# A streaming log-softmax: two places at which SyncE empties its store queue before the next load

## The chip, the cores and the metric

One NeuronCore of one Trainium2 chip runs the kernel. The metric is the device time of one execution in microseconds (us); the figure for a kernel is the median of several runs. A separate, profiled execution gives the trace that the views below come from.

## The reference

The input x is float32 of shape 16 x 512 x 50000: 8192 rows of 50000 values, 1.64 GB. The result has the same shape.

```python
def reference(x: np.ndarray) -> np.ndarray:
    max_x = np.max(x, axis=-1, keepdims=True)
    shifted = x - max_x
    log_sum_exp = np.log(np.sum(np.exp(shifted), axis=-1, keepdims=True))
    return (shifted - log_sum_exp).astype(np.float32)
```

## The kernel before

**Tiles.** A tile is 32 rows. Each row is cut into 4 parts of 12500 values, and each part lies on a partition of its own, so that a tile fills 128 partitions x 12500 float32 (50,000 bytes per partition, 6.4 MB). There are 256 tiles and 4 buffers of that size (`bufs[0]` to `bufs[3]`); tile t lives in buffer t mod 4. A tile is loaded, worked on in place, and stored from the same buffer.

**What happens to a tile.** VectorE waits for the load (`landed[j]`, L45 called by `whole`). It takes the negated maximum of each partition in 4 pieces of 3125 columns (L206). While it does, ScalarE takes the exponential of each finished piece with that piece's maximum as the bias, and sums it (L242). VectorE brings the 4 partitions of a row to one maximum with two small transposes (L174 to L189). ScalarE makes the factors that bring the pieces' sums to that maximum (L250), VectorE multiplies (L217), TensorE adds the 4 partitions of a row with a matrix of ones (L270), ScalarE takes the logarithm (L236), and VectorE subtracts maximum and logarithm from the whole tile in one pass (L194), which increments `subtracted[j]`. For the last tile this pass is made in 4 pieces.

**Who issues the transfers.** All loads and stores are issued by SyncE, in an order written out by hand, on one hardware queue that feeds 16 DMA engines; each engine carries 8 of the 128 partitions of every transfer. A load (L145) increments `landed[j]` by 16, one for each DMA engine; a store (L149) first waits for `subtracted[j]` and increments `stored[j]` by 16. `take` (L43 to L45) waits until a semaphore has a value and takes that value off again.

**The order.** SyncE loads tiles 0 to 3 and stores tile 0. Then come 63 rounds of 4 steps each (L155 to L160). Step j of round q stores tile 4q + 1 + j from the next buffer k, waits until the store from buffer j (tile 4q + j) has landed, and loads tile 4q + 4 + j into buffer j:

```python
            for j in range(NBUF):
                k = (j + 1) % NBUF
                store(k, dst(q, j), bufs[k])
                take(sync, stored[j])
                load(j, src(q, j))
```

After the rounds SyncE stores tiles 253 and 254, stores tile 255 in 4 pieces of 12500 bytes per partition, and waits for the stores that are still under way. The other engines have loops of their own of 63 rounds; only the semaphores tie them to SyncE.

Of the kernel before, what the change touches and what calls it, by code (L numbers as in the profile page):

```python
# [17 lines left out]
R = P // G  # L18
C = 3125
NBUF = 4  # L20

NS = 4

# [19 lines left out]
def take(engine, sem, n=16):  # L43

    engine.wait_ge(sem, n).then_inc(sem, -n)  # L45


def cols(c):
    return slice(c * C, (c + 1) * C)
# [3 lines left out]
def kernel(  # L53
# [11 lines left out]
    ntiles = N // R  # L65


    rounds = (ntiles - NBUF) // NBUF
    assert ntiles % NBUF == 0 and rounds >= 2

    xt = xf.rearrange("(t r) (g w) -> t (r g) w", r=R, g=G)
    ot = of.rearrange("(t r) (g w) -> t (r g) w", r=R, g=G)

    def run(a, first, n):

        part = a[first : first + NBUF * n].rearrange("(q i) p w -> q i p w", i=NBUF)
        return lambda q, i: part[bass.ds(q, 1), i].rearrange("o p w -> (o p) w")
# [12 lines left out]
    ones = consts.tile([P, P], FP32, name="ones")  # L90
    bufs = [data.tile([P, W], FP32, name=f"buf{j}") for j in range(NBUF)]
    dump = dump_pool.tile([P, C], FP32, name="dump")
    sums = sum_pool.tile([P, NBUF], FP32, name="sums")
    rowsums = [sums[:, k : k + 1] for k in range(NBUF)]

# [15 lines left out]
    def sem(name):  # L111
        return ctx.enter_context(nc.semaphore(name))

    landed = [sem(f"landed{j}") for j in range(NBUF)]
    stored = [sem(f"stored{j}") for j in range(NBUF)]
# [13 lines left out]
    @block.gpsimd  # L129
    def _(gpsimd):  # L130
        view = ones.rearrange("p (r g) -> p r g", g=G)
        gpsimd.memset(ones, 1.0).then_inc(ready)  # L132
        gpsimd.affine_select(  # L133
            out=view, in_=view, pattern=[[-G, R], [0, G]], base=0,
            channel_multiplier=1, compare_op=ALU.is_ge, fill=0.0,
        ).wait_op(ready, 1, "sem-ge").then_inc(ready)
        gpsimd.affine_select(  # L137
            out=view, in_=view, pattern=[[G, R], [0, G]], base=G - 1,
            channel_multiplier=-1, compare_op=ALU.is_ge, fill=0.0,
        ).wait_op(ready, 2, "sem-ge").then_inc(ready)  # L140

    @block.sync
    def _(sync):
        def load(j, src):
            sync.dma_start(out=bufs[j], in_=src).then_inc(landed[j], 16)  # L145

        def store(j, dst, buf):
            take(sync, subtracted[j], 1)
            sync.dma_start(out=dst, in_=buf).then_inc(stored[j], 16)  # L149

        for t in range(NBUF):
            load(t, xt[t])
        store(0, ot[0], bufs[0])
        src, dst = run(xt, NBUF, rounds), run(ot, 1, rounds)
        with sync.Fori(0, rounds) as q:  # L155
            for j in range(NBUF):
                k = (j + 1) % NBUF
                store(k, dst(q, j), bufs[k])
                take(sync, stored[j])
                load(j, src(q, j))  # L160
        for j in range(1, NBUF - 1):
            store(j, ot[ntiles - NBUF + j], bufs[j])
        for c in range(NS):
            store(NBUF - 1, ot[ntiles - 1][:, cols(c)], bufs[NBUF - 1][:, cols(c)])
        for j in range(NBUF - 1):
            take(sync, stored[j])
        take(sync, stored[NBUF - 1], 16 * NS)
# [147 lines left out]
```

## Time and profile before

| | us |
|---|---|
| median of 5 runs | 7593.89 |
| lowest and highest of the 5 | 7593.56, 7594.41 |
| the profiled execution | 7595.35 |
| its span, from the first to the last instruction | 7593.6 |
| VectorE busy (72% of the span) | 5440.7 |
| ScalarE busy (42%) | 3184.7 |
| TensorE busy (6%) | 477.9 |
| one load, from issue to landing, median | 44.2 |
| one store, from issue to landing, median | 47.8 |

How to read it: the page first gives the busy time of each engine and then the span in 40 equal slices, where a digit is the busy share of a slice in tenths; the DMA line is the mean busy share of the 16 DMA engines, and the GB/s line is what they moved. HBM is read with 1638.40 MB and written with 1638.40 MB, which is 432 GB/s over the span. In a line on a group of instructions, the name after L is a line of the kernel, `out<-in` are its tiles, and behind the bar stand the busy time, the mean length of one in ns, and the idle time of the engine just before them, with what ended it. DVE is VectorE, ACT ScalarE, PE TensorE, SP SyncE; a name with a q (DVEq, SPq) is that engine's sequencer. The line on the chain of waits follows the work that ended last back from the end; in this execution it covers only the last 46 us, from 7547.38 to the end of the last pass of VectorE.

### The profile page before, as it was taken

Reading aid. Unit: us, or ns where it says so; the run is one execution under the profiler, and the core shown is the slowest. Engines: PE = TensorE matmul, PEld = TensorE weight load, DVE = VectorE, ACT = ScalarE, POOL = GpSimd, SP = SyncE. Lnnn points to the kernel's source line nnn. Section 1 sums busy time; section 2 is a strip of 40 time slices with the busy share of each in tenths; the row PEclk is TensorE's granted clock in tenths of the full one; section 3 lists DMA queues with packets and bytes.
Section 4 is the critical chain, followed back from the end, with each engine's and each line's share of the span. In section 5 each row is a group of like instructions: output and inputs, shape, how many; then the busy total and the mean of one; then the engine's idle time right before and its main releaser. Section 6 shows DMA issues by size and latency. Waiting matters only on the chain. (4 is left out here: it accounts for less than half of the span.)

```text
span 7593.6 us, 14139 instructions
## 1 busy us (share of the span) xinstructions
PE 477.9 (6%) x2048; PEld 456.0 (6%) x2048; DVE 5440.7 (72%) x2819; ACT 3184.7 (42%) x2561; POOL 1.4 (0%) x7
## 2 busy tenths in 40 slices
PE   0000000000000000000000000000000000000000
PEld 0000000000000000000000000000000000000000
DVE  7777777777777777777777777777777777777776
ACT  4444443434444344443444434444344443444433
POOL 0000000000000000000000000000000000000000
DMA  9999999999999999999999999999999999999998
GB/s 425 431 432 433 432 433 433 434 432 433 433 434 432 433 434 433 432 433 433 433 432 433 433 432 433 433 433 433 432 433 434 433 432 432 434 433 432 432 434 386
DMA packets 74162, 3276.85 MB, mean 432 GB/s; under 512 B 8240, under 2 KB 8240, under 8 KB 8240
## 3 DMA queue, kind: packets, MB, share of 16 engines
q1 hardware_dynamic: 74160, 3276.83, 99.9%
q14 instruction: 2, 0.02, 0.0%
HBM read 1638.40 MB, written 1638.40 MB: 432 GB/s over the span
## 5 line engine op out<-in xcount | busy, mean ns | idle before, releaser
L242 ACT ACTIVATE dump<-buf,negm 128x3125 f32<-128x3125 f32 x1024 | 2937.2, 2868 | 3806.3 <-DVE negm L206 3708.8
L206 DVE TENSOR_REDUCE negm<-buf 128x1 f32<-128x3125 f32 x1024 | 3418.3, 3400 | 924.6 <-DVEq L45 924.6
L194 DVE TENSOR_SCALAR buf<-buf,negmax,logsum 128x12500 f32<-128x12500 f32 (+1 forms) x259 | 1738.9, 6715 | 553.8 <-ACT logsum L236 553.8
L270 PE MATMUL sums<-scaled,ones 128*128 128x1 f32 x2048 | 477.9, 355 | 7088.5 <-DVE scaled L217 7088.5
L270 PEld LDWEIGHTS sums<-scaled,ones 128*128 128x128 f32 x2048 | 456.0, 328 | 7110.4 <-DVE scaled L217 7110.4
L217 DVE TENSOR_TENSOR scaled<-scale,part 128x4 f32<-128x4 f32 x256 | 41.7, 163 | 580.2 <-ACT scale L250 580.2
L236 ACT ACTIVATE logsum<-sums 128x1 f32<-128x1 f32 x256 | 43.9, 171 | 551.0 <-PE sums L270 551.0
L242 ACT ACTIVATION_READ_ACCUMULATOR dump<-buf,negm 128x1 f32 x1024 | 190.8, 186 | 0.0
L250 ACT ACTIVATE scale<-negm,negmax 128x4 f32<-128x4 f32 x256 | 76.1, 297 | 23.6
L211 DVE TENSOR_REDUCE negp<-negm 128x1 f32<-128x4 f32 x256 | 40.2, 157 | 39.2 <-DVE negm L206 39.2
L189 DVE STREAM_TRANSPOSE negmax<-spread 128x32 f32<-128x32 f32 x256 | 54.2, 212 | 8.9
L174 DVE STREAM_TRANSPOSE allneg<-negp 128x32 f32<-128x32 f32 x256 | 54.2, 212 | 8.9
L177 DVE TENSOR_REDUCE rowneg<-allneg 128x8 f32<-128x32 f32 x256 | 47.6, 186 | 8.9
L183 DVE COPY spread<-rowneg 128x32 f32<-128x32 f32 x256 | 46.3, 181 | 8.9
L257 ACT ACT_TABLE_LOAD x1 | 1.3, 1283 | 1.0 <-SPq L109 1.0
L133 POOL TENSOR_SCALAR_AFFINE_SELECT ones<-ones 128x128 f32<-128x128 f32 x1 | 0.5, 520 | 0.1
L137 POOL TENSOR_SCALAR_AFFINE_SELECT ones<-ones 128x128 f32<-128x128 f32 x1 | 0.5, 519 | 0.1
L132 POOL MEMSET ones<- 128x128 f32 x1 | 0.2, 205 | 0.5 <-SPq L109 0.5
L299 POOL MEMSET const-bfloat16-1.0<- 128x1 bf16 x1 | 0.1, 102 | 0.0
L299 POOL MEMSET const-uint8-127<- 128x1 uint8 x1 | 0.1, 102 | 0.0
L299 POOL MEMSET const-float32-0.0<- 128x1 f32 x1 | 0.1, 99 | 0.3 <-issue 0.3
L299 POOL MEMSET const-float32-1.0<- 128x1 f32 x1 | 0.1, 99 | 0.0
## 6 DMA issues: line engine op xcount, KB each, us to landing
buf<-in_x_dram SPq DMA_DIRECT2D x256, 6250.0 KB, 44.2
out_dram<-buf SPq DMA_DIRECT2D x255, 6250.0 KB, 47.8
out_dram<-buf SPq DMA_DIRECT2D x4, 1562.5 KB, 11.7
```

The costliest lines, as they stand in the source:

```text
L174: vector.transpose(out=allneg, in_=negp.to_broadcast([P, SQ]))
L177: vector.tensor_reduce(out=rowneg, in_=allneg.rearrange("p (r g) -> p r g", g=G), op=ALU.min, axis=AX,)
L183: vector.tensor_copy(out=spread.rearrange("p (r g) -> p r g", g=G), in_=rowneg[:, :, None].to_broadcast([P, SQ // G, G]),)
L189: vector.transpose(out=negmaxs[k], in_=spread)
L194: ins = vector.tensor_scalar(out=buf, in0=buf, scalar1=negmaxs[k][:, 0:1], scalar2=logs[k], op0=ALU.add, op1=ALU.subtract,)
L206: vector.tensor_reduce(out=negms[j][:, c : c + 1], in_=bufs[j][:, cols(c)], op=ALU.max, axis=AX, negate=True,).then_inc(shifted.sem if c < ...
L211: vector.tensor_reduce(out=negp, in_=negms[j], op=ALU.min, axis=AX).then_inc(on_dve.sem)
L217: vector.tensor_mul(out=scaleds[j], in0=scales[j], in1=parts[j])
L236: scalar.activation(out=logs[k], in_=rowsums[k], func=ACT.Ln)
L242: scalar.activation(out=dump, in_=bufs[j][:, cols(c)], func=ACT.Exp, bias=negms[j][:, c : c + 1], scale=1.0, accum_out=parts[j][:, c : c + 1],
L250: scalar.activation(out=scales[j], in_=negms[j], func=ACT.Exp, bias=negmaxs[j][:, 0:1], scale=-1.0,)
L270: ins = tensor.matmul(rowsums[j], ones, scaleds[j][:, c : c + 1], start=c == 0, stop=c == NS - 1,)
```

## The change

The 63 rounds are cut into three stretches of 21. The first round of the second and of the third stretch is built apart. In its first step (j = 0), SyncE stores tile 4q + 1, waits until the store from buffer 0 has landed, and then waits as well until the store that it has just issued, from buffer 1, has landed; only then it loads buffer 0. In the second step of that round the wait for the store from buffer 1 is left out, since it was already taken. These rounds are q = 21 and q = 42, so the loads concerned are those of tiles 88 and 172. All other rounds run as before, in loops of 21, 1, 20, 1 and 20 rounds in place of one loop of 63. Nothing but SyncE's code differs.

```diff
+STRETCHES = 3
...
-    assert ntiles % NBUF == 0 and rounds >= 2
+    assert ntiles % NBUF == 0 and rounds % STRETCHES == 0
...
-        src, dst = run(xt, NBUF, rounds), run(ot, 1, rounds)
-        with sync.Fori(0, rounds) as q:
-            for j in range(NBUF):
-                k = (j + 1) % NBUF
-                store(k, dst(q, j), bufs[k])
-                take(sync, stored[j])
-                load(j, src(q, j))
+        def stretch(done, n, settled):
+            src, dst = run(xt, NBUF * (done + 1), n), run(ot, NBUF * done + 1, n)
+            with sync.Fori(0, n) as q:
+                for j in range(NBUF):
+                    k = (j + 1) % NBUF
+                    store(k, dst(q, j), bufs[k])
+                    if not (settled and j == 1):
+                        take(sync, stored[j])
+                    if settled and j == 0:
+                        take(sync, stored[k])
+                    load(j, src(q, j))
+
+        part = rounds // STRETCHES
+        stretch(0, part, False)
+        for i in range(1, STRETCHES):
+            stretch(part * i, 1, True)
+            stretch(part * i + 1, part - 1, False)
```

## The prediction

> **What bounds the kernel now.** I read the busy shares and the slices first, then the waits, then SyncE's own order of transfers, then the end of the run in small windows.
>
> The page's parts 1 to 3, and the groups of its part 5 that carry the idle time:
>
> ```profile
> PE 477.9 (6%) x2048; PEld 456.0 (6%) x2048; DVE 5440.7 (72%) x2819; ACT 3184.7 (42%) x2561; POOL 1.4 (0%) x7
> ...
> DMA  9999999999999999999999999999999999999998
> GB/s 425 431 432 433 432 433 433 434 432 433 433 434 432 433 434 433 432 433 433 433 432 433 433 432 433 433 433 433 432 433 434 433 432 432 434 433 432 432 434 386
> ...
> q1 hardware_dynamic: 74160, 3276.83, 99.9%
> ...
> L206 DVE TENSOR_REDUCE negm<-buf 128x1 f32<-128x3125 f32 x1024 | 3418.3, 3400 | 924.6 <-DVEq L45 924.6
> ```
>
> No compute engine is full; the 16 DMA engines are, in every slice, at 432 to 434 GB/s. VectorE waits 924.6 us in 249 tiles (3.7 us each) for a load to land. So the transfers set the time: 256 loads and 256 stores of 6.4 MB on one queue.
>
> Around the first place that the change touches, SyncE's timeline (start, length, line, transfer) reads:
>
> ```profile
> 2506.31 0.34 SPq L149 DMA_DIRECT2D out_dram<-buf  x1
> 2524.80 0.35 SPq L145 DMA_DIRECT2D buf<-in_x_dram  x1
> 2536.06 0.34 SPq L149 DMA_DIRECT2D out_dram<-buf  x1
> 2554.43 0.35 SPq L145 DMA_DIRECT2D buf<-in_x_dram  x1
> 2565.67 0.34 SPq L149 DMA_DIRECT2D out_dram<-buf  x1
> 2584.07 0.35 SPq L145 DMA_DIRECT2D buf<-in_x_dram  x1
> ```
>
> The pace is 29.63 us for a load and a store, 14.8 us each. The load at 2554.43 goes out as the store issued at 2506.31 lands (47.8 us is the median of a store to landing). At that moment the load of 2524.80 (44.2 us to landing: 2569.0, and VectorE starts on it at 2569.11) and the store of 2536.06 (lands 2583.9) are still queued: **29.6 us of work stands in the queue** whenever SyncE issues a load.
>
> One more thing decides the price of emptying it: the 16 DMA engines are not abreast. The end of the run in windows (window, length, busy per engine, clock, DMA share, GB/s):
>
> ```profile
> 7560.00:7569.00 9.00, 1.87 (x8) 1.78 (x8) 4.28 (x9) 3.99 (x6) 0.00 (x0) 1.00 0.05 22
> 7569.00:7584.50 15.50, 0.00 (x0) 0.00 (x0) 5.01 (x3) 0.00 (x0) 0.00 (x0) 1.00 0.98 414
> 7584.50:7591.50 7.00, 0.00 (x0) 0.00 (x0) 0.00 (x0) 0.00 (x0) 0.00 (x0) 1.00 0.06 27
> ```
>
> A share of 0.05 to 0.06 is one engine of 16, at 22 to 27 GB/s. Fifteen engines have nothing left at 7560 and again at 7584.5; one is behind. The trace's landing records (one per DMA engine and transfer) say the same for the whole run: between first and last engine lie 3.7 us at 1200 us, 7.3 at 2584, 13 at 4990, 20 at the end, while the first 15 stay within 3.7. One engine loses 0.076 us per tile, evenly. SyncE's loads show it too: 29.56 us apart from 540.83 to 1191.21, 29.63 from there on, when that engine has become the last. The end hangs on **the slow engine's queue**, which never empties; the lead of the other 15 (under 29.6 us) buys nothing.
>
> **The change part by part.** Removed: nothing but one wait per drain (the second load's, already taken). Added: twice, before the loads of tiles 88 and 172 (today issued at 2554.43 and near 5044), a wait for the store issued just before. Moved behind that wait: at the first place the load of tile 88, the store of tile 86 (today 2565.67) and the load of tile 89 (today 2584.07).
>
> *The wait.* It ends when the store of 2536.06 lands, 2583.9. The load of 2524.80 is ahead of that store, so the queue is then empty. SyncE goes from a landing to its next issue in 0.22 us (landing record against the issue row), so tile 88 is issued at 2584.1, not 2554.43; the store of tile 86 (its VectorE work ends at 2565.4) and the load of tile 89 follow within about 1.5 us (three issues of 0.34 to 0.35 and the steps between). Before the wait the slow engine did exactly the work that it does today until 2583.9. **The delay of 29.7 us is therefore not the price**; the price is the gap in the slow engine's stream, from its last store packet to its first load packet, and slower first packets.
>
> *The gap, from both sides.* The trace has no load issued into an empty queue in mid-run, but two restarts. The first load: issued 1.04, VectorE starts on it at 19.06, 18.02 us later, against 14.78 for a load in a full queue (half of 29.56): at most 3.2 us extra on the last engine; the landing record of the first engine gives 16.71, 1.9 extra. The last stores: issued 7568.65, 15 engines are done at 7584.5 (row above), 15.9 us for what takes 14.78: 1.1 extra. With SyncE's 0.22 the gap is 1.3 to 3.5 us; I take the load row at its lower side, 2.1, since a load restarts here too.
>
> *After the restart.* When all 16 engines start abreast, they lose something more until they have settled: at the start of the run the first engine's landings fall 1.4 us behind a pace of 14.78 within 20 transfers, the slow engine about 0.65 more (its straight line of 0.076 us per tile carried back to the start), the worst engine 3.7. I take 1.4; bounds are 0 and 3.7.
>
> *What hides the rest.* The three transfers issued together are 44 us of work. The store of tile 87 (its load lands as today, VectorE ends at 2595.1) is issued about 2595.3, long before they are through. The next load is issued when the store of tile 86 lands, two transfers after the restart, with a load and a store queued: the pattern of today, with the same 29.6 us of cover. VectorE is late by the gap, has 3.7 us of idle time per tile, and its store is due only some 30 us later. If that cover were gone, each us of lateness would cost one. The new loops' register and branch steps on SyncE, and their code, stand where SyncE waits 11 to 18 us per transfer anyway: nothing, and if the cover were gone, under 1 us.
>
> *Sum.* 2 x (2.1 + 1.4) = 7.0 us. The profiled execution takes 7595.35 us (span 7593.6 and 1.7 around it), so 7602.4; on the median of the runs, 7593.89, it is **7600.9 us**, 0.09% more. Ends: 2 x 1.3 = 2.6 (7596.5) and 2 x (3.5 + 3.7) = 14.4 (7608.3).
>
> *A rule that speaks against the change.* The trace shows 0.9 us from the last stores' issue to their first packets, and 1.1 to 3.2 us extra for a transfer into an idle queue. The Trainium skill, DMA: Bandwidth & Descriptors, "Anatomy of one DMA — SWDGE (gpsimd) path", puts a fixed cost of some 2.0 us on each DMA (fitted on GpSimd's path, not SyncE's), and its "Rules for kernel authors" advise issuing early so that this overlaps; by it, each drain lays one such cost bare and the change costs an estimated 4.0 us, 7597.9.
>
> **The rivals.**
>
> *The engines share one ceiling.* Then what 15 engines idle while the slow one catches up is lost, not only the slow one's gap. Its place is the last microseconds before 2583.9. The lead over the slow engine is some 6 us against the middle engine at the first drain (7.3 less 1.1), and 84 tiles later again (84 x 0.076 = 6.4). Price 15/16 x 6 x 2 = 11.3, with the 7.0: 18.3 us, 7612.2, slower by 0.24%. For it: the total stands at 433 GB/s whatever the mix of loads and stores, as a common limit would. Against it: alone, the slow engine makes 27 GB/s (last row above), one sixteenth of 433; a shared ceiling would have let it run faster. It decides if the other engines' idle time is not made good later, that is, if the pace after the drain is no better than 29.63.
>
> *The slow engine is slow because it lags.* Then abreast it keeps the early pace. At 29.56 for all 168 tiles after the first drain it gains 168 x 0.076 = 12.8, less 7.0: 5.8 us faster, 7588.1, still within 0.2%. For it: the loads really are 29.56 apart up to 1191. Against: the slow engine's lag grows by the same 0.92 us per 12 tiles at a lag of 5 and of 19 us, so the lag does not make it slow; the early pace is that of another engine, which was last then.
>
> *The change does nothing*, if the queue were never empty at the wait. Against it: a load is issued only behind the wait, and nothing else feeds the queue. 7593.9.
>
> **How the numbers follow.** The forecast, two gaps on the slow engine, 7600.9: 82%. Shared ceiling, 7612.2: 8%. Pace regained, 7588.1: 6%. Nothing: 2%. The last 2% are for costs or gains not seen here. The range takes the forecast's bounds, 7596.5 to 7608.3; the rest may lie outside. A change of under 0.2% (15.2 us) is about what a measurement of this kernel cannot tell from none. Forecast, pace regained and nothing lie within it; the shared ceiling is slower. The high bounds of the forecast come near 15 us, and a regained pace with a cheap restart would come near it from below: faster 3%, same 87%, slower 10%.
>
> **What would show it.** In the changed profile: SyncE issues a load near 2584.1 and, within 1.5 us, a store and a load; the same near 5077. Just before each, a few us with a DMA share of 0.06; then a stretch of 1 to 2 us with nothing. VectorE's wait for tile 88 is near 6 us, 2 to 3 over its usual 3.7. Afterwards the loads are 29.56 apart for some 35 to 40 tiles and then 29.63, and the end shows one engine behind by about 7 us, not 17 to 20. If the slow engine's share before the drain rises well over 0.06, engines do share a limit and the gap is cheaper than its idle time. If loads stay at 29.56 to the end, its slowness came from its lag. If gaps over 5 us follow a drain, the refill is not covered as worked out.

## The result, and the profile after

The changed kernel takes **7603.25 us** (median of 29 runs, 7599.49 to 7606.72) against 7593.93 us before (median of 49 runs, 7592.9 to 7597.39): 9.3 us more, a ratio of 1.0012 with a 95% interval of 1.0007 to 1.0017. That lies within 0.2%, and the forecast was 7.0 us more. The profiled execution takes 7605.97 us, 10.6 more than the one before; its span is 7604.2.

The page after, the lines that answer to those of before:

```profile
PE 477.9 (6%) x2048; PEld 456.0 (6%) x2048; DVE 5440.6 (72%) x2819; ACT 3184.7 (42%) x2561; POOL 1.4 (0%) x7
...
GB/s 424 431 433 433 431 432 433 431 433 432 433 433 433 416 429 432 432 432 433 433 433 433 433 433 433 433 408 432 430 432 433 433 432 433 433 433 433 433 433 419
...
q1 hardware_dynamic: 74160, 3276.83, 99.9%
...
L217 DVE TENSOR_REDUCE negm<-buf 128x1 f32<-128x3125 f32 x1024 | 3418.3, 3401 | 935.1 <-DVEq L46 935.1
```

Every engine does the same work in the same time. Two slices of the GB/s line have dips, 416 and 408, and the slice behind the first is still low (429); they hold the two places. VectorE's wait for loads grows from 924.6 to 935.1 us, by 10.5 of the 10.6 us between the profiled executions.

SyncE's timeline at the first place (start, length, line, transfer):

```profile
2524.67 0.35 SPq L146 DMA_DIRECT2D buf<-in_x_dram  x1
2535.79 0.34 SPq L150 DMA_DIRECT2D out_dram<-buf  x1
2583.80 0.35 SPq L146 DMA_DIRECT2D buf<-in_x_dram  x1
2584.26 0.36 SPq L150 DMA_DIRECT2D out_dram<-buf  x1
2584.67 0.43 SPq L146 DMA_DIRECT2D buf<-in_x_dram  x1
2595.04 0.33 SPq L150 DMA_DIRECT2D out_dram<-buf  x1
2618.06 0.34 SPq L146 DMA_DIRECT2D buf<-in_x_dram  x1
```

The load of tile 88 goes out at 2583.80, 48.0 us after the store that it waits for, and the store and the load behind it follow within 0.9 us. The load of tile 90 follows 34.3 us after that of tile 88; two transfers at the pace of 14.78 would be 29.6.

Now the DMA engines around it, in windows (window, length, busy time of each engine, clock, DMA share, GB/s). A window counts a packet, with its bytes and its whole time, where the packet starts, so the share of a short window can be over 1; the lengths of single packets, given below, are the firmer reading.

```profile
2579.50:2583.00 3.50, 0.00 (x0) 0.00 (x0) 3.28 (x4) 3.12 (x3) 0.00 (x0) 1.00 0.07 29
2583.25:2584.70 1.45, 0.00 (x0) 0.00 (x0) 0.27 (x2) 1.45 (x1) 0.00 (x0) 1.00 0.00 0
2587.00:2598.00 11.00, 0.91 (x5) 0.82 (x4) 6.79 (x1) 0.17 (x1) 0.00 (x0) 1.00 1.01 436
2598.00:2602.00 4.00, 0.00 (x0) 0.00 (x0) 0.00 (x0) 0.00 (x0) 0.00 (x0) 1.00 1.18 375
```

First the last engines finish their store (share 0.07), one of 16 alone from 2581.8 on, then for 1.45 us none works, then all 16 run at full pace, and then, at 2598 to 2602, all are busy but move only 375 GB/s. This last row was not in the prediction. The trace's records of single packets show what it is: in this stretch each of the 16 engines takes 2.6 to 3.4 us for one packet, where a packet of 50,000 bytes takes 1.85 us in steady work. It is the last packet of the load of tile 88, where the queue turns from a load to a store. In the execution before, the same is seen once, at 59.8 us, where the four first loads end and the first store begins (2.4 to 3.2 us on all 16), and nowhere in steady work.

**Where the time went**, from the load issues of the two profiled executions. Tile by tile, the changed kernel is 0.1 us ahead at tile 87, 4.4 us late at tile 90, 6.9 at tile 104, 7.0 at tile 171; from tile 104 to 171 its loads are 29.63 us apart, as those of before are. At the second place it goes from 7.0 to 11.2 (tile 174) and 14.5 (tile 194). From there it *regains* 3.9 us, down to 10.55 at tile 255, since its loads are now 29.57 us apart (tiles 243 to 255: 354.83 us for 12) where those of before are 29.63 apart. Late in the changed kernel, SyncE's timeline has

```profile
7158.91 0.35 SPq L146 DMA_DIRECT2D buf<-in_x_dram  x1
7170.21 0.34 SPq L150 DMA_DIRECT2D out_dram<-buf  x1
7188.45 0.35 SPq L146 DMA_DIRECT2D buf<-in_x_dram  x1
7199.73 0.34 SPq L150 DMA_DIRECT2D out_dram<-buf  x1
7218.01 0.35 SPq L146 DMA_DIRECT2D buf<-in_x_dram  x1
```

with loads 29.54 and 29.56 us apart, the pace that the kernel before had only up to 1191 us.

### The profile page after: what moved, and what is told of

Same layout as the page of the kernel before. It is cut to its first block, busy times and chain, and to the rows that moved or that the text cites. A ratio compares the mean times of both kernels' runs of the same rounds, so it can differ in the third digit from the quotient of the medians.

```text
span 7604.2 us, 14111 instructions
## 1 busy us (share of the span) xinstructions
PE 477.9 (6%) x2048; PEld 456.0 (6%) x2048; DVE 5440.6 (72%) x2819; ACT 3184.7 (42%) x2561; POOL 1.4 (0%) x7
## 5 line engine op out<-in xcount | busy, mean ns | idle before, releaser
L217 DVE TENSOR_REDUCE negm<-buf 128x1 f32<-128x3125 f32 x1024 | 3418.3, 3401 | 935.1 <-DVEq L46 935.1
## 6 DMA issues: line engine op xcount, KB each, us to landing
out_dram<-buf SPq DMA_DIRECT2D x4, 1562.5 KB, 14.5
```

The source lines that it names most:

```text
L217: vector.tensor_reduce(out=negms[j][:, c : c + 1], in_=bufs[j][:, cols(c)], op=ALU.max, axis=AX, negate=True,).then_inc(shifted.sem if c < ...
```

## The experiments

Each was timed beside the kernel before on the same chip, and the difference is from that kernel's median there, which differs by up to 1.7 us between chips. In the cuts of code, `...` stands for lines left out; the five loops of the changed kernel are written out with their numbers. The theory at first: a drain costs what the slow engine stands idle, and some refilling. The rivals: 15 engines' idle time is lost as well (shared ceiling), or it is the code or the order of the issues that costs.

**The loops alone.** The five loops of the changed kernel, without the added waits:

```diff
...
-            stretch(part * i, 1, True)
-            stretch(part * i + 1, part - 1, False)
+        stretch(0, 21, False)
+        stretch(21, 1, False)
+        stretch(22, 20, False)
+        stretch(42, 1, False)
+        stretch(43, 20, False)
```

> SyncE's code is cut into the same five loops as in the changed kernel, but no wait is added. If the cost lies in the slow engine's gap and the restart that follows it: 7593.9 us, as before (within 1). If the engines share one ceiling: the same, since nothing is drained. If the new loops and their code cost something: up to 7603.

Measured 7594.11 us against 7593.74: 0.4 more, ratio 1.0001 (0.9992 to 1.0010). The new code costs nothing that can be told in the total. One small thing of it can be seen in the trace: between tiles 91 and 93, where the third loop begins, the loads fall 0.7 us back. There a packet of 8192 bytes of the queue that the page calls instruction takes 0.31 us at 2686.88, and the packet of 50,000 bytes that starts as it ends takes 2.13 us.

**The wait behind the load.**

```diff
-                    if settled and j == 0:
-                        take(sync, stored[k])
                     load(j, src(q, j))
+                    if settled and j == 0:
+                        take(sync, stored[k])
```

> The same two extra waits for the store in flight, but each put behind the load of tiles 88 and 172 instead of ahead of it, so that a whole load (14.8 us) still stands in the queue when the wait ends. Slow engine's gap: no gap, 7594 us (within 1.5). Shared ceiling: no engine idles, 7594 as well. If it is the waiting itself, or the store and load delayed behind it, that costs: 7598 to 7603.

Measured 7594.67 against 7593.74: 0.9 more, ratio 1.0003 (0.9994 to 1.0012); four of the 11 runs lie at 7597 to 7601, which stays unexplained. The same wait on the same store, one line lower, is all but free as long as a load stands in the queue. So the waiting and the delay of the store behind it are not the cost; the empty queue is.

**One late drain.**

```diff
...
+        stretch(0, 59, False)
+        stretch(59, 1, True)
+        stretch(60, 3, False)
```

> One drain only, as in the changed kernel, but late: before the load of tile 240, where the last engine is some 18 us behind the others. Slow engine's gap: the price of one drain does not depend on the lead, one gap and part of a restart: 3.5 to 6 us, 7597.5 to 7600. Shared ceiling: 15/16 of a lead of 17 to 18 us is lost as well: 7613 to 7616.

Measured 7599.41 against 7593.74: 5.7 more, ratio 1.0008 (0.9999 to 1.0017). In its trace 15 engines are 13 to 17 us ahead of the last just before the drain (landing records near 7080 us), against 1.4 to 5.3 us at the changed kernel's first drain. A shared ceiling would have lost that lead, 7613 or more. It falls: the fast engines' idle time is free.

**Three quarters of the store.** The slow engine is to keep work while the others run dry.

```diff
...
+                        sync.dma_start(
+                            out=dst(q, j)[:, : 3 * C], in_=bufs[k][:, : 3 * C]
+                        ).then_inc(most, 16)
+                        sync.dma_start(
+                            out=dst(q, j)[:, 3 * C :], in_=bufs[k][:, 3 * C :]
+                        ).then_inc(stored[k], 16)
+                        take(sync, stored[j])
+                        take(sync, most)
...
```

> The store before the wait is issued as two transfers, three quarters and one quarter of the columns, and the extra wait ahead of the load is for the larger one alone. The slow engine then still has a quarter of a store (3.7 us) queued when the load goes out, while engines that are further ahead run dry. Slow engine's gap: no gap on it, so 7594 to 7597 us, the upper end if the restart of the others costs the slow one something. Shared ceiling: the middle engine idles about 1 us at the first place and 4 at the second, 15/16 of that is lost: 7598 to 7600.

Measured 7600.99 against 7593.74: 7.3 more, ratio 1.0010 (1.0001 to 1.0019). **Here my theory fell short**: the slow engine had no gap and the cost was there all the same. The packet records show its last store packet ending at 2582.05 and its first load packet starting at 2582.06 and taking 1.85 us, and yet it lost 2.1 us within that load. Its windows:

```profile
2579.00:2582.00 3.00, 0.00 (x0) 0.00 (x0) 2.74 (x5) 2.62 (x3) 0.00 (x0) 1.00 0.89 300
2582.00:2593.00 11.00, 1.87 (x8) 1.78 (x8) 6.54 (x4) 2.58 (x4) 0.00 (x0) 1.00 1.01 436
2593.00:2597.00 4.00, 0.00 (x0) 0.00 (x0) 0.64 (x1) 0.00 (x0) 0.00 (x0) 1.00 1.20 375
```

The restart is at 2579 to 2582, then the pace is full, and at 2593 to 2597 comes the row with 375 GB/s of the changed kernel again. The slow engine is in it with the others: its packets there take 3.0 and 2.8 us, 2.1 more than two at 1.85. So there are two costs: the gap, and the **first turn from load to store after the engines ran dry**, which all 16 make within about 1 us of each other. In steady work of the kernel before, the first 15 engines are spread over 3.7 us, two packets (11 of them within 1.3 us), with the slow one further behind, and no such turn is seen. My theory from here on was that the turn is slow because the engines make it together.

**Two loads first.** If it is the turn, it must move with the turn.

```diff
-                    store(k, dst(q, j), bufs[k])
                     if not (settled and j == 1):
+                        store(k, dst(q, j), bufs[k])
                         take(sync, stored[j])
...
                     load(j, src(q, j))
+                    if settled and j == 1:
+                        store(k, dst(q, j), bufs[k])
```

> The changed kernel, but after each of the two waits the loads of two tiles go out before the store that stood between them. Theory now: a drain costs the slow engine's gap, and then a slow turn from load to store that all 16 engines make together (their packets of 1.85 us take about 3 us there in the changed kernel, 13.5 us after the restart). By it the slow packets move with the turn, one transfer later (some 28 us after the restart), and the sum stays: 7601 to 7606 us. If instead they come at a fixed time after a restart, they stay at 13.5 us. If the turn were free, the sum would fall to two gaps: 7598 to 7600.

Measured 7607.53 against 7595.40: 12.1 more, ratio 1.0015 (1.0006 to 1.0024). The load of tile 88 goes out at 2585.02. Its windows:

```profile
2588.00:2600.00 12.00, 1.14 (x6) 1.05 (x5) 6.79 (x1) 0.17 (x1) 0.00 (x0) 1.00 1.03 446
2600.00:2614.00 14.00, 0.00 (x0) 0.00 (x0) 11.17 (x4) 7.08 (x5) 0.00 (x0) 1.00 0.97 418
2614.00:2618.00 4.00, 0.00 (x0) 0.00 (x0) 3.14 (x6) 3.62 (x3) 0.00 (x0) 1.00 1.13 375
```

Nothing happens at 2598 to 2602 now; the row with 375 GB/s stands at 2614 to 2618, at the end of the second load (its 16 slow packets start at 2614.4 to 2615.3 and take 2.4 to 3.2 us). It moved with the turn. The sum is over the expected range and 2.8 us over that of the changed kernel; which part of the new order costs that was not followed up.

That the engines turn together is not enough, though. In the changed kernel they make the next turn from load to store near 2629 us, still within 1.2 us of each other by the landing records (0.7 at the slow turn), and twelve of its 16 packets take 1.87 us or less, the other four 2.0 to 2.2:

```profile
2629.00:2633.00 4.00, 0.00 (x0) 0.00 (x0) 0.27 (x1) 0.00 (x0) 0.00 (x0) 1.00 1.00 425
```

Later delays stand at turns from store to load as well: near 2674 us, 22 packets take 2.0 to 2.5 us. What the runs show is that the first turn from load to store after a restart is slow on all 16 engines; what sets it apart from the second is not shown.

**One quarter of the store**, the control for the split: the same edit with `: C` and `C :` in place of `: 3 * C` and `3 * C :`.

> As the run with three quarters, with the same split of the store in two, but the first transfer is one quarter of the columns and the extra wait is for that one. When it ends, the slow engine has 11 us queued and the other engines still have some 7 (first place) and 3 (second): none runs dry, so they are not brought abreast. Gap and shared turns: no cost, 7594 to 7596 us. If the split of the store, or the wait, is what cost 7.2 us in the run with three quarters: 7599 to 7602.

Measured 7599.95 against 7595.20: 4.8 more, ratio 1.0006 (0.9997 to 1.0015). Taken alone, the sum lies in the range expected for a costly split or wait, and outside that for gap and turns. The two places speak otherwise. At the first, no engine ran dry, and the cost was nothing: the loads are 0.77 us behind those of the profile before at tile 87, and 0.75 at tile 91. At the second the lead had not been taken back by the first, and was 8 to 13 us over the 15 others, not the 8 over all of them that I had counted with, so engines did run dry:

```profile
2573.00:2580.00 7.00, 0.00 (x0) 0.00 (x0) 7.00 (x4) 6.03 (x5) 0.00 (x0) 1.00 1.02 439
...
5061.00:5064.50 3.50, 0.00 (x0) 0.00 (x0) 3.50 (x2) 1.25 (x1) 0.00 (x0) 1.00 0.53 229
...
5078.00:5082.00 4.00, 0.75 (x4) 0.66 (x4) 3.01 (x1) 0.17 (x1) 0.00 (x0) 1.00 1.08 375
```

The first row is the first place, at full pace. The other two are the second: a dip in which only the slow engine and the stragglers work, and 16 us on the row with 375 GB/s once more. From the landing records, the first 15 engines lay 5.0 us apart before and 1.7 after it; the slow one stayed 9 us behind, was never idle, and still lost 2.1 us by tile 186. So the split and the wait are free at the first place; where engines run dry and come abreast there is a cost, even for an engine that did not run dry. The rest of the sum comes where the edit does nothing. The 0.8 us near tile 92 are those of the loops alone: the third loop begins there, and a packet of 8192 bytes of the instruction queue at 2678.68 stands just ahead of the one packet of 2.26 us. The 2.3 us between tiles 186 and 229 stay open.

**A longer gap.**

```diff
                         take(sync, stored[k])
+                        sync.wait_ge(subtracted[NBUF - 1], 1)
```

> The changed kernel with a further wait at the same two places, until VectorE has subtracted in tile 87 (171), 11.3 us after the store has landed. Gap and shared turns: the empty stretch gets 11.3 us longer for all engines, the restart is the same, so 2 x 11.3 on top of the changed kernel: 7626 (7622 to 7630). If empty time of the queue is partly made good later, or hidden by VectorE's 3.7 us of idle time in a tile: clearly less, under 7618.

Measured 7628.82 against 7595.20: 33.6 more, ratio 1.0044 (1.0030 to 1.0057). In its trace the load goes out 59.2 us after the store, against 48.0: 11.2 longer, twice 22.3, and the sum is 24.3 over that of the changed kernel. Within the spread of these runs (5 us), empty time of all 16 engines goes into the total one for one, and VectorE's idle time hides none of it.

**One early drain**, before tile 36 (`stretch(0, 8, False)`, `stretch(8, 1, True)`, `stretch(9, 54, False)`).

> One drain only, before the load of tile 36, where the engines lie within 4 us of each other and the engine that is slow later is not yet last. Gap and turns: about the price of the late single drain (7599.4), 7597 to 7601, since neither depends on the lead. If a drain pays by putting the slow engine abreast: less than that the smaller the lead to regain, so at most 7594. Shared ceiling: the middle engine's lead of some 3 us more than a gap, 7599 as well; it is the late drain that spoke on that.

Measured 7603.21 against 7595.40: 7.8 more, ratio 1.0010 (1.0001 to 1.0019), over the range expected for gap and turns and on the far side of a gain. One drain in the first eighth of the run costs nearly as much as the change's two.

**Twenty drains**, one every 12 tiles.

> Twenty drains, one every 12 tiles, in place of two. Gap and turns: 4.6 us a drain as in the changed kernel gives 7687; 6.8 a drain (what the load times of the changed kernel lose within 12 tiles of the first drain), less some 16 us of drift that no longer counts because other engines are last, gives 7714: 7680 to 7720. Gap alone (2.1 to 2.9 a drain): 7636 to 7652.

Measured 7743.55 against 7595.40: 148.2 more, ratio 1.0194 (1.0180 to 1.0208), 7.4 us a drain. That is above my range too (7720), and three times what the gap alone would give. Its trace shows why: after the drain near 2629 us the loads go out at 2663.31, 2693.15 and so on to 2932.68, nine steps of 29.9 us on average up to the next drain. The engines hardly come back to the pace of 29.56 before they are emptied again.

**Sparing one engine.** The kernel before, where in round 61 the store of tile 245 goes out in two parts:

```diff
...
+                        for part in (slice(0, 120), slice(120, P)):
+                            sync.dma_start(
+                                out=dst(q, j)[part], in_=bufs[k][part]
+                            ).then_inc(stored[k], 16)
...
```

> The kernel before, without drains, but the store of tile 245 is issued as two transfers, of 120 and of 8 partitions. The Trainium skill (DMA: Bandwidth & Descriptors, section Why a DMA increments its semaphore by 16 and not by 1) says that 120 partitions run on the 15 lowest-numbered DMA engines and 8 on the lowest 8, so engine 15 is spared 8 packets of 1.85 us. If one engine's queue sets the end and it is engine 15: 7579 to 7584 us. If the slow engine is another: up to one packet more, 7593 to 7597. If no single engine sets the end: 7593 to 7597 as well.

Measured 7605.42 against 7595.40 (7600.7 to 7621.1): 10.0 more, ratio 1.0017 (1.0008 to 1.0026). As a measure of what a spared engine is worth it is **inconclusive**. The windows of its trace after the split store was issued at 7279.32:

```profile
7280.00:7300.00 20.00, 0.06 (x1) 0.07 (x1) 14.47 (x10) 12.26 (x9) 0.00 (x0) 1.00 1.04 420
7300.00:7310.00 10.00, 1.80 (x8) 1.72 (x8) 6.79 (x1) 0.17 (x1) 0.00 (x0) 1.00 0.99 285
7310.00:7320.00 10.00, 0.00 (x0) 0.00 (x0) 7.49 (x3) 3.73 (x3) 0.00 (x0) 1.00 0.99 275
```

The engines are busy but move 275 to 285 GB/s while the split store runs, two thirds of the usual pace, with many packets of 3.5 to 4 us, and the engines end up spread over 34 us. What one engine might have been spared drowns in that.

The landing records still tell whether the spared engine is the slow one. Of the two stores' increments, 23 come from 7311.57 on, which is 15 and 8 engines, and two already at 7279.86 and 7280.25, as the stores were issued. The load issued at 7268.19, ahead of them, lands on 15 engines by 7299.21 and on the slow one at 7312.37. The load issued behind them, at 7297.70, lands on one engine at 7315.49, 12 us before any other: that is the spared engine, which had no store between. It cannot be the slow one, since a load takes an engine 14.8 us and only 3.1 lie between 7312.37 and 7315.49. So in this execution the slow engine is another than the spared one; which, and whether it is always the same, stays open.

## Why the prediction was right, and where it was not

*What bounds the kernel; the 29.7 us of waiting are not the price.* Right. Two waits behind the load cost 0.9 us, the same two ahead of it 9.3. (The GB/s slices are not all at 432 to 434, as I read them: the first two are 425 and 431, the last 386. Nothing rests on that.)

*The gap: 1.3 to 3.5 us, 2.1 taken.* Right. At the first place the last store packet ends at 2583.21, the load is issued at 2583.80, the first load packets start at 2584.75 to 2585.25 and take 2.3 to 2.9 us in place of 1.85: 2.1 to 2.9 us, by engine. The longer gap shows that such time counts in full.

*After the restart: 1.4 us, bounds 0 and 3.7.* **This is the term that was mis-sized.** At the first place a drain costs 7.0 us and not 3.5, so the restart takes 4.1 to 4.9, over its upper bound. I had it from the lag of the engines over the first 20 transfers of the run. The start of the run shows its first slow turn at 59.8 us, which I did not look at packet by packet. The first turn from load to store after the restart costs 0.8 to 1.5 us at once; smaller delays, packets of up to 2.6 us on some of the engines, follow at turns of both kinds until about 3080 us, while the engines spread again. The changed kernel is 4.4 us late two tiles after the drain and 6.9 fourteen tiles later. Three quarters of the store has this term without the gap: 7.3 us for two places.

*A term that I left out.* The slow engine stops being the last when others have lost more than it in a restart. I had named the better pace among the signs (29.56 for 35 to 40 tiles after a drain) and not put it into the sum. After the first drain it did not come: from tile 104 on the loads are 29.63 apart. After the second it held to the end, the loads stay 29.57 apart, and 3.9 us come back. With it the sum closes: 7.0 + 7.5 - 3.9 = 10.6 us, as between the two profiled executions. The end shows no engine 7 us behind: the last landing records of whole transfers lie within 4.4 us. In the landing records one engine does fall back over the last 48 tiles, from 1.6 us behind the first at 6075 us to 4.35 at 7494, 0.057 a tile, so an engine nearly as slow is still there. That the forecast of 7.0 came as near to 9.3 as it did was luck: this term and the one above have opposite signs. Three quarters of the store, with no gap, is only 2.0 us cheaper than the change for the same reason: its loads are 29.63 apart to the end.

*What hides the rest: VectorE and SyncE.* Right: the loops alone cost 0.4 us, and no later transfer waited for a late store. Only VectorE's wait for tile 88 was 7.6 us and not near 6, since the slow packets of the turn are in that load.

*Shared ceiling, 7612.2.* Wrong, by the late drain. *Pace regained, 7588.1.* Wrong as a gain, by the early drain (7.8 us more): a reset of the engines pays for nothing, though a part of what it describes, 3.9 us, was there. *Does nothing:* wrong; the queue is empty for some 1.5 us.

*The rule of the Trainium skill.* One fixed cost of about 2.0 us a drain, fitted on GpSimd's path, from "Anatomy of one DMA — SWDGE (gpsimd) path" of DMA: Bandwidth & Descriptors, is close to the gap measured here on SyncE's queue (2.1 to 2.9 us). It does not cover the restart, and the 4.0 us that I worked out by it are under half of what was measured.

**What stays open:** why the first turn from load to store after a restart is slow, and the next one hardly (shown are its place, its length, that it moves with the turn and that it hits an engine that was not idle; that turning together is the cause was argued and is not borne out by the second turn); which engine is the slow one, and why; and why the runs of the changed kernel spread over 7 us, where most of those of before lie within 3.

## What to carry to other kernels

Where transfers are the bound, as here, a wait of the issuing engine costs next to nothing as long as a transfer still stands in the queue when it ends, and the full empty time once none does: put such a wait behind the issue of the next transfer, not ahead of it. A queue that runs dry costs more than its gap, since the turns after the restart are slow too; the gap was 2 to 3 us here, and a single drain 5.7 to 7.8. Read a lag between DMA engines from where the last one stands: idle time on the others was free, and bringing them into step was a loss.

## What was not expected of the hardware

- The first turn from load to store after the queue was empty takes 2.4 to 3.4 us a packet on all 16 DMA engines in place of 1.85, 375 GB/s over 4 us in place of 433. The second, 30 us later in the changed kernel, takes 1.87 us or less on twelve of them.
- One DMA engine ran 0.25% slower than the 15 others, evenly over some 6 ms (0.076 us a tile of 29.6), and alone set the end.
- While a store of 120 partitions and one of 8 ran, the engines moved 275 to 285 GB/s, against 433 with transfers of 128.
- A packet of 8192 bytes of the instruction queue among the data packets, where a new loop of SyncE begins, went with a delay of 0.7 us in the loads.
